# A block of three branches in emulated fp32: weights two chunks ahead, attention results summed where they arise, other load orders at four borders, last group in halves

## The chip, the cores and the metric

The kernel runs on one core of a Trainium2 chip. Times are device microseconds (us) of a whole execution. TensorE is called PE, VectorE DVE, ScalarE ACT, GpSimd POOL, and SyncE SP; SP here issues most loads, one queue in program order.

## The reference

One layer of a hybrid encoder, 512 positions by 2048 features, fp32:

```
h = rms_norm(x); proj = h @ w_in            # 2048 x 15424: all branch inputs and gates
conv_y = b * conv3(c * u);   o_conv = (conv_y * silu(conv_z)) @ w_conv_out
q = rms_norm(c_q) @ w_uq;  kv = rms_norm(c_kv) @ w_ukv   # 16 heads, chunk-causal attention
                             o_mla  = (mla_y * silu(mla_z)) @ w_mla_out
mem_y = cross-attention of 4 heads into 256 memory tokens
                             o_mem  = (mem_y * silu(mem_z)) @ w_mem_out
merged = sig(g_conv)*o_conv + sig(g_mla)*o_mla + sig(g_mem)*o_mem
out = x + merged @ w_o
```

## The kernel before

**Arithmetic.** A product in fp32 is made of three matmuls in fp32r (mm3, L158 to L163): high by high, low by high, high by low. So each operand is split into a high and a low part: ACT rounds the raw tile to the high part, DVE subtracts it for the low part. For activations the splits are made once; for weights they are made as they are streamed.

**Weights.** A weight chunk is loaded by SP into a raw tile (tag raw, 3 buffers of 8 KB a partition) and split into whi (ACT) and wlo (DVE), two buffers each. The wide matrices w_in, w_mla_out and w_o go through a fast scheme with 7 instead of 8 block products: pair_weights (L245 to L257) loads four blocks, makes three sums on DVE (L250 to L252), then whi (L254) and wlo (L255), each 128 x 1792. The activations need such sums too: pair_parts (L235 to L242), of a pair of feature blocks. One chunk is 42 matmuls of 256 columns (panel_steps); four chunks make a panel of 256 output features. The plain matrices (w_ukv, w_uq, w_conv_out, w_mem_out) go through plain_jobs and dense_units, at 384 or 512 columns, with splits at L154 and L155.

**Queue of jobs.** Every chunk is a job in one list. take (L172) runs the job of the chunk it returns and of the next: load, sums and splits of chunk n+1 are written into the program before the matmuls of chunk n.

**Order of the work.** The order of PE and SP is the order in which the program is written; for the other engines a scheduler picks among what is ready (in the first panels the order of DVE is written too). Streams of attention and projection are interleaved by strings such as ORDER_Q1 and ORDER_MEM, in which a letter or digit is a step of one stream and w a step of the projection.

**Stages**, by time in the profile:

- 0 to 115: keys and values of the memory tokens; norm of x and its pairs xp.
- 115 to 1355: 60 panels of w_in. A finished panel e is sent to DRAM (latdram, zdram, gdram and others) after its non-linearity; panel cq also gives the rotary keys.
- 1355 to 1650: the latent projections (w_ukv, w_uq) and attention of 16 heads, two heads a group. The latents come back from latdram as blk tiles; krh, krl, tabs, mask are small tables. attend multiplies a head's result by its gate z and stores it to aadram (L960, L961).
- 1600 to 1780: w_conv_out, with the attention into the memory tokens between its chunks.
- 1790 to 1955: panels of w_mla_out. Their activations xm are made by new_pairs (L1138): load from aadram into a raw tile, three sums, split.
- 1955 to 2044: w_mem_out in 4 groups of 512 features. mem_pair (L1190) merges two of its banks with the sum of the other branches and makes the pair xo: loads from gdram and mgdram into a raw tile, L1195 (product), L1196 (sum), three sums, split at L241 (ACT) and L242 (DVE).
- 2044 to the end: panels of w_o on the xo pairs.

Of the kernel before, what the change touches and what calls it, by code (L numbers as in the profile page):

```python
# [30 lines left out]
P = 128  # L31
S = 512
# [75 lines left out]
def body(ctx, tc, a, out):  # L108
# [63 lines left out]
    def take(ahead=1):  # L172
        for entry in queue[:1 + ahead]:
            if entry[1] is None:
                entry[1] = entry[0]()
        return queue.pop(0)[1]

    def plain_jobs(srcs, n, cut=False, parts=(), beside=None):
# [56 lines left out]
    def pair_parts(f, x):  # L235
# [3 lines left out]
        vec.tensor_tensor(out=f[:, 7], in0=f[:, 3], in1=f[:, 6], op=ALU.add)  # L239
        yield  # L240
        act.activation(x[:, 0], f[:, 1:8], AF.Copy)  # L241
        vec.tensor_tensor(out=x[:, 1], in0=f[:, 1:8], in1=r32(x[:, 0]), op=ALU.subtract)  # L242
        yield

    def pair_weights(src):  # L245
# [10 lines left out]
        return hi, lo  # L256

    later = []

    def panel_steps(xp, e, tag, middle=None):  # L260
# [5 lines left out]
        for c in range(nch):  # L266
# [6 lines left out]
            for kk in range(2):  # L273
# [81 lines left out]
    kr_ = const.tile([P, NTB], F32, name="kr_")  # L355
    pos_i = const.tile([P, NTB], I32, name="pos_i")
# [16 lines left out]
    aadram = dram.tile([NP, P, 2, S], F32, name="aadram")  # L373
# [238 lines left out]
    def rotary():  # L612
# [68 lines left out]
        krr = rstd_of(krss, NTB, 1.0 / 64, const)  # L681
# [19 lines left out]
        pool.tensor_tensor(out=kr_, in0=lmean[:, 0], in1=mhalf[:, :NTB], op=ALU.pow)  # L701
        yield
# [8 lines left out]
    def finish(n, e):  # L711
# [43 lines left out]
    queue.insert(next(at for at in range(len(queue)) if at == 12), [rotary_weights, None])  # L755
# [47 lines left out]
    tabs = pc.tile([P, 2, NTB, 64], F32, name="tabs")  # L803
# [89 lines left out]
    run("28w", w=first)  # L893

    def attend(head, h, qrb, kn, vs, qn, qd):
# [59 lines left out]
        z = pa.tile([P, S], F32, tag="z", name="z", bufs=2)  # L955
        nc.sync.dma_start(z, zdram[head // 2][:, head % 2])
# [3 lines left out]
        vec.tensor_tensor(out=z, in0=yb, in1=z, op=ALU.mult)  # L960
        nc.gpsimd.dma_start(aadram[head // 2][:, head % 2], z)  # L961
# [218 lines left out]
    for _ in work:  # L1180
        next(pairs, None)
# [139 lines left out]
```

## Time and profile before

| what | value |
|---|---|
| median of 3 runs | 2218.77 us (2218.43 to 2224.96) |
| profiled execution, own time | 2227.57 us |
| its span | 2225.8 us |
| mean granted clock of PE | 0.981 |
| PE / DVE / ACT / POOL busy | 2151.9 / 1746.5 / 1005.0 / 116.0 us |
| DMA | 328.02 MB, mean 147 GB/s |

The span is that of the profiled execution; the 1.8 us beside it lie around the first and last instruction. A row of a timeline is: start in us, duration in us, engine, line, operation, what it writes and reads, shape, count; in brackets the idle time of the engine before it and what ended that. A count over 1 merges neighbours, and the duration is then from the first start to the last end. SPq is SP's queue of DMA issues: the duration of an issue row is not that of the transfer.

### The profile page before, as it was taken

How to read it: one execution, taken by the hardware profiler on the slowest of the kernel's cores; microseconds unless marked ns; L12 is line 12 of the kernel's file. 1: busy time of each engine (PE TensorE's matmuls, PEld its weight loads, DVE VectorE, ACT ScalarE, POOL GpSimd, SP SyncE). 2: the span in 40 equal slices, each digit the busy share in tenths (PEclk: the TensorE clock that was granted, in tenths of full speed). 3: DMA queues.
4: the chain of work that ended last, by engine and by line, in shares of the span. 5: the costliest groups of instructions: out<-in, count | busy, mean ns of one | idle time of the engine just before them, and what ended most of it. 6: DMA issues, size and time to landing. Idle time of an engine off the chain costs nothing.

```text
span 2225.8 us, 38861 instructions
## 1 busy us (share of the span) xinstructions
PE 2151.9 (97%) x16040; PEld 2059.5 (93%) x16040; DVE 1746.5 (78%) x2759; ACT 1005.0 (45%) x1215; POOL 116.0 (5%) x157
## 2 busy tenths in 40 slices
PE   9989999999999999999999998999999879999998
PEld 8779999999999999999999997888888679987898
DVE  6866788888888888888888874788876778857886
ACT  6633344343344334444444444777765333323332
POOL 0000000000000000000000001222211100000000
PEclk9989999999999999999999999999999989999999
DMA  8533343343333334344444345222246746654443
GB/s 329 204 103 124 133 149 117 124 142 124 124 125 132 124 124 136 120 134 138 133 135 144 130 133 214 73 74 100 93 178 225 254 145 171 209 189 161 153 160 114
DMA packets 92993, 328.02 MB, mean 147 GB/s; under 512 B 10960, under 2 KB 11216, under 8 KB 90768
## 3 DMA queue, kind: packets, MB, share of 16 engines
q1 hardware_dynamic: 75600, 264.90, 35.5%
q0 software_dynamic: 8288, 35.39, 4.7%
q10 hardware_dynamic: 8928, 25.25, 3.2%
q8 instruction: 125, 2.05, 0.4%
q14 instruction: 52, 0.43, 0.1%
HBM read 270.19 MB, written 55.31 MB: 146 GB/s over the span
## 4 chain that ended last, share of the span: by engine, by line
PE 75%; DVE 8%; DMA 6%; issue 6%; ACT 3%; POOL 1%; SPq 0%; DVEq 0%; ACTq 0%; POOLq 0%
PE acc L162 13%; PE acc L161 13%; PE acc L163 13%; PE aux L162 10%; PE aux L163 10%; PE aux L161 10%; DVE wlo L255 3%; DMA raw<-in_w_o 1%; ACT whi L254 1%; DMA raw<-in_w_mla_out 1%; DMA raw<-in_w_h 1%; PE aux L943 1%; DVE wlo L155 1%; DVE raw L250 1%; DMA raw<-gdram 1%
## 5 line engine op out<-in xcount | busy, mean ns | idle before, releaser
L254 ACT ACTIVATE whi<-raw 128x1792 fp32r<-128x1792 f32 x304 | 517.5, 1703 | 792.9 <-PE acc L162 363.9
L255 DVE TENSOR_TENSOR wlo<-raw,whi 128x1792 fp32r<-128x1792 f32 x304 | 614.7, 2023 | 205.8 <-ACT whi L254 205.3
L161 PE MATMUL acc<-xp,whi 128*128 128x256 f32 (+1 forms) x1712 | 481.1, 281 | 5.5 <-ACT whi L254 3.2
L163 PE MATMUL acc<-xp,wlo 128*128 128x256 f32 (+1 forms) x1712 | 480.7, 281 | 3.1 <-DVE wlo L255 3.1
L162 PE MATMUL acc<-xp,whi 128*128 128x256 f32 (+1 forms) x1712 | 481.1, 281 | 0.0
L163 PE MATMUL aux<-xp,wlo 128*128 128x256 f32 x1680 | 471.3, 281 | 4.2 <-DVE wlo L255 3.8
L161 PE MATMUL aux<-xp,whi 128*128 128x256 f32 x1680 | 471.3, 281 | 1.2 <-ACT whi L254 1.2
L162 PE MATMUL aux<-xp,whi 128*128 128x256 f32 x1680 | 471.5, 281 | 0.0
L161 PEld LDWEIGHTS acc<-xp,whi 128*128 128x128 f32 (+1 forms) x1712 | 322.6, 188 | 6.2 <-ACT whi L254 3.6
L163 PEld LDWEIGHTS acc<-xp,wlo 128*128 128x128 f32 (+1 forms) x1712 | 321.5, 188 | 3.8 <-DVE wlo L255 3.7
L162 PEld LDWEIGHTS acc<-xp,whi 128*128 128x128 f32 (+1 forms) x1712 | 322.0, 188 | 0.0
L163 PEld LDWEIGHTS aux<-xp,wlo 128*128 128x128 f32 x1680 | 316.3, 188 | 5.6 <-DVE wlo L255 5.6
L161 PEld LDWEIGHTS aux<-xp,whi 128*128 128x128 f32 x1680 | 317.6, 189 | 1.5 <-ACT whi L254 1.4
L162 PEld LDWEIGHTS aux<-xp,whi 128*128 128x128 f32 x1680 | 317.1, 189 | 0.0
L250 DVE TENSOR_TENSOR raw<-raw 128x512 f32<-128x512 f32 x304 | 208.5, 686 | 58.3 <-DMA raw<-in_w_h 32.8
L155 DVE TENSOR_TENSOR wlo<-raw,whi 128x1024 fp32r<-128x1024 f32 (+2 forms) x87 | 101.3, 1165 | 53.0 <-ACT whi L154 53.0
L154 ACT ACTIVATE whi<-raw 128x1024 fp32r<-128x1024 f32 (+2 forms) x87 | 88.0, 1013 | 104.4 <-PE acc L162 43.9
L252 DVE TENSOR_TENSOR raw<-raw 128x256 f32<-128x256 f32 x304 | 128.1, 422 | 6.2
L251 DVE TENSOR_TENSOR raw<-raw 128x256 f32<-128x256 f32 x304 | 128.0, 421 | 5.7
L161 PE MATMUL acc<-whi,blk 128*128 128x384 f32 (+1 forms) x224 | 86.3, 385 | 7.6 <-ACT whi L154 7.6
L319 POOL TENSOR_TENSOR rs_r<-rs_t,mhalf 128x2 f32<-128x2 f32 (+2 forms) x71 | 70.0, 997 | 313.6 <-DVE rs_t L318 199.4
L162 PE MATMUL acc<-wlo,blk 128*128 128x384 f32 (+1 forms) x224 | 82.0, 366 | 0.3 <-DVE wlo L155 0.3
(345 smaller groups left out, 3922.8 us busy)
## 6 DMA issues: line engine op xcount, KB each, us to landing
raw<-in_w_h SPq DMA_DIRECT2D x240, 512.0 KB, 3.5
raw<-in_w_mla_out SPq DMA_DIRECT2D x32, 512.0 KB, 3.6
raw<-in_w_o SPq DMA_DIRECT2D x32, 512.0 KB, 3.8
raw<-in_w_mem_kv SPq DMA_DIRECT2D x31, 512.0 KB, 7.5
gdram<-e ACTq DMA_DIRECT2D x24, 512.0 KB, 2.9
raw<-in_w_ukv SPq DMA_DIRECT2D x16, 512.0 KB, 4.9
raw<-in_w_conv_out SPq DMA_DIRECT2D x16, 512.0 KB, 6.1
raw<-in_w_mem_out SPq DMA_DIRECT2D x16, 512.0 KB, 4.5
```

The costliest lines, as they stand in the source:

```text
L154: act.activation(hi[:, cols], raw[:, cols], AF.Copy)
L155: vec.tensor_tensor(out=lo[:, cols], in0=raw[:, cols], in1=r32(hi[:, cols]), op=ALU.subtract)
L161: nc.tensor.matmul(o, lhsT=s[0], rhs=m[0], start=start, stop=False, skip_group_check=shared)
L162: nc.tensor.matmul(o, lhsT=s[0], rhs=m[1], start=False, stop=False, skip_group_check=shared)
L163: nc.tensor.matmul(o, lhsT=s[1], rhs=m[0], start=False, stop=stop, skip_group_check=shared)
L250: vec.tensor_tensor(out=f[:, 4:6], in0=f[:, 1:3], in1=f[:, 0:1].to_broadcast([P, 2, 256]), op=ALU.add)
L251: vec.tensor_tensor(out=f[:, 6], in0=f[:, 5], in1=f[:, 1], op=ALU.add)
L252: vec.tensor_tensor(out=f[:, 7], in0=f[:, 6], in1=f[:, 3], op=ALU.add)
L254: act.activation(hi, f[:, 1:8], AF.Copy)
L255: vec.tensor_tensor(out=lo, in0=f[:, 1:8], in1=r32(hi), op=ALU.subtract)
L319: pool.tensor_tensor(out=r, in0=t, in1=mhalf[:, :n], op=ALU.pow)
L943: nc.tensor.transpose(out=b[:, i * P:(i + 1) * P], in_=ps[i][:, j * P:(j + 1) * P], identity=ident)
```

## The change

- **take** keeps two steps per job: load and sums of chunk n+2 are written ahead of the splits of chunk n+1 (jobs are generators with two yields).
- **Rotary keys** (rotary_keys_raw) move from the end of panel cq to the middle of the next panel, on the other bank tag; the weights w_kr go from place 12 to 15 of the list. mqs and mqn, constants for the memory queries, are made in that stage and no more in the memory attention.
- **Border to the latents:** krh, krl, tabs, mask and w_uq are loaded ahead of the last two latent blocks; ORDER_Q1 and ORDER_MEM are rewritten.
- **Latent results:** z is one tile for two heads (one buffer), the three sums of a pair are made there, and the 7 blocks (128 x 1792) are stored to aadram. new_pairs loads them into the xm tile and splits in place: no raw tile, no sums.
- **w_mem_out** runs in groups of 512, 512, 512, 256 and 256; mem_pair has a tile mg of its own (one buffer) in place of a raw tile.

The core of the diff:

```diff
     def take(ahead=1):
-        for entry in queue[:1 + ahead]:
+        for at, entry in enumerate(queue[:2 + ahead]):
             if entry[1] is None:
                 entry[1] = entry[0]()
-        return queue.pop(0)[1]
+                entry.append(next(entry[1]))
+            if at <= ahead and entry[2] is None:
+                entry[2] = next(entry[1])
+        return queue.pop(0)[2]
...
+            if c == 2:
+                while between:
+                    between.pop(0)("aux" if tag == "acc" else "acc")
...
             if i == 0:
-                rotary_keys_raw("acc")
+                between.append(rotary_keys_raw)
...
-    run("4w", w=first)
-    for n in (6, 7):
-        latent(n)
     nc.sync.dma_start(r32(krh), krdram[:, 0])
...
-    run("28w", w=first)
+    run("9w", w=first)
+    for n in (6, 7):
+        latent(n)
+    run("23w", w=first)
...
-        z = pa.tile([P, S], F32, tag="z", name="z", bufs=2)
-        nc.sync.dma_start(z, zdram[head // 2][:, head % 2])
+        if h == 0:
+            z = pa.tile([P, 8, H], F32, tag="z", name="z", bufs=1)
+            nc.sync.dma_start(two(z), zdram[head // 2])
...
-        nc.gpsimd.dma_start(aadram[head // 2][:, head % 2], z)
+        if h == 1:
+            pair_sums(z)
+            nc.gpsimd.dma_start(aadram[head // 2], z[:, 1:8])
...
-            x, t = pair_tile(px, f"xm{n}"), raw_tile()
-            nc.sync.dma_start(flat(t[:, 0:4]), aadram[n].rearrange("p f n -> p (f n)"))
+            x = pair_tile(px, f"xm{n}")
+            nc.sync.dma_start(r32(x[:, 1]), aadram[n])
             xp.append(x)
-            yield from pair_parts(t, x)
+            yield
+            pair_split(r32(x[:, 1]), x)
+            yield
...
-    for grp in range(4):
+    for grp in range(3):
         upcoming(*plain_jobs([a["w_mem_out"][grp][c] for c in range(4)], 512))
+    for grp in range(2):
+        upcoming(*plain_jobs([a["w_mem_out2"][grp][c] for c in range(4)], 256))
...
     def mem_pair(n, banks):
-        t = raw_tile()
+        t = pm.tile([P, 8, H], F32, tag="mg", name="mg", bufs=1)
...
-    for grp in range(4):
-        if grp == 3:
+    for tag, width in (("acc", 512), ("aux", 512), ("acc", 512), ("aux", 256), ("aux", 256)):
+        if done == 7:
             work = panels(xp, a["w_o"], 8, lambda n: make_o(n), lambda n, e: finish_o(n, e))
```

How the order moves at three places. Lines shift by a few: L249, L250 to L252, L255 and L242 of before are L262, L263 to L265, L269 and L250 of the change.

DVE in the first panels of w_in, before. e is a pair of x being scaled (L458) and summed (L236 to L239), raw the weights:

```order
L255 TENSOR_TENSOR wlo<-raw,whi 128x1792
L458 TENSOR_TENSOR e<-e,xscale 128x1024
L236 TENSOR_TENSOR e<-e 128x512
L237 SCALAR_TENSOR_TENSOR e<-e 128x256
L239 TENSOR_TENSOR e<-e 128x256
L250 TENSOR_TENSOR raw<-raw 128x512
```

And the change:

```order
L269 TENSOR_TENSOR wlo<-raw,whi 128x1792
L263 TENSOR_TENSOR raw<-raw 128x512
L264 TENSOR_TENSOR raw<-raw 128x256
L265 TENSOR_TENSOR raw<-raw 128x256
L477 TENSOR_TENSOR e<-e,xscale 128x1024
L243 TENSOR_TENSOR e<-e 128x512
L244 SCALAR_TENSOR_TENSOR e<-e 128x256
```

The sums of the next weights stand right behind the split, and the four operations on x behind them.

SP at the border from the panels to the latents, before:

```order
L795 DMA blk<-latdram 128x1024 x8
L889 DMA krh<-krdram 128x512
L890 DMA krl<-krdram 128x512
L891 DMA tabs<-csdram 128x512
L892 DMA mask<-in_mask 128x512
L191 DMA raw<-in_w_uq 128x768 x2
```

And the change:

```order
L822 DMA blk<-latdram 128x1024 x6
L913 DMA krh<-krdram 128x512
L914 DMA krl<-krdram 128x512
L915 DMA tabs<-csdram 128x512
L916 DMA mask<-in_mask 128x512
L196 DMA raw<-in_w_uq 128x768 x2
L822 DMA blk<-latdram 128x1024 x2
```

Two blocks go behind w_uq. The semaphore of the last gate panel's write (DMAHW0), on which the seventh block waited, is waited for by krl in the change.

SP from the memory output to w_o, before (gdram and mgdram are the loads of a merge pair; the rows start with the last w_mem_out load):

```order
L191 DMA raw<-in_w_mem_out 128x1024 x2
L1192 DMA raw<-gdram 128x1024
L1193 DMA raw<-mgdram 128x1024
L249 DMA raw<-in_w_o 128x1024 x2
L1192 DMA raw<-gdram 128x1024
L1193 DMA raw<-mgdram 128x1024
```

And the change:

```order
L196 DMA raw<-in_w_mem_out 128x512 x4
L1225 DMA mg<-gdram 128x1024
L1226 DMA mg<-mgdram 128x1024
L1225 DMA mg<-gdram 128x1024
L1226 DMA mg<-mgdram 128x1024
L262 DMA raw<-in_w_o 128x1024 x3
```

The first three loads of w_o follow the loads of the sixth and seventh merge pair, where before the first two followed those of the sixth alone.

## Rows read from the trace of the kernel before

**Rows 1.** The page: busy time of PE, and the groups of weight splits and weight sums of the panels (busy us in all, mean ns of one, idle time before them).
```profile
PE 2151.9 (97%) x16040; PEld 2059.5 (93%) x16040; DVE 1746.5 (78%) x2759; ACT 1005.0 (45%) x1215; POOL 116.0 (5%) x157
...
L254 ACT ACTIVATE whi<-raw 128x1792 fp32r<-128x1792 f32 x304 | 517.5, 1703 | 792.9 <-PE acc L162 363.9
L255 DVE TENSOR_TENSOR wlo<-raw,whi 128x1792 fp32r<-128x1792 f32 x304 | 614.7, 2023 | 205.8 <-ACT whi L254 205.3
...
L250 DVE TENSOR_TENSOR raw<-raw 128x512 f32<-128x512 f32 x304 | 208.5, 686 | 58.3 <-DMA raw<-in_w_h 32.8
...
L252 DVE TENSOR_TENSOR raw<-raw 128x256 f32<-128x256 f32 x304 | 128.1, 422 | 6.2
```

**Rows 2.** Busy time by stage: stretch, its length, busy us (and instructions) of PE, PEld, DVE, ACT, POOL, the granted clock of PE, DMA share, GB/s.
```profile
115.00:225.00 110.00, 97.28 (x719) 94.95 (x719) 75.53 (x99) 40.42 (x37) 1.94 (x4) 0.89 0.32 106
225.00:1355.00 1130.00, 1128.72 (x9588) 1127.99 (x9587) 935.05 (x1293) 474.80 (x360) 11.86 (x20) 1.00 0.41 134
...
1430.00:1650.00 220.00, 217.71 (x1257) 194.17 (x1256) 179.10 (x515) 166.57 (x405) 51.67 (x60) 1.00 0.30 102
1750.00:1800.00 50.00, 34.05 (x154) 27.96 (x153) 40.61 (x49) 17.11 (x13) 4.35 (x8) 0.83 0.68 242
1960.00:2040.00 80.00, 80.00 (x355) 66.26 (x354) 51.92 (x59) 24.65 (x20) 0.85 (x1) 1.00 0.56 190
2040.00:2140.00 100.00, 89.25 (x688) 86.67 (x687) 81.16 (x106) 34.03 (x24) 0.00 (x0) 0.95 0.45 148
```

**Rows 3.** The same table for short stretches at the borders.
```profile
125.00:175.00 50.00, 40.62 (x284) 38.99 (x283) 38.30 (x49) 17.79 (x15) 0.00 (x0) 0.86 0.21 66
215.00:220.00 5.00, 4.77 (x27) 4.77 (x28) 1.72 (x4) 0.00 (x0) 0.00 (x0) 0.66 0.35 105
1370.00:1380.00 10.00, 4.84 (x14) 4.44 (x15) 1.92 (x2) 3.12 (x8) 0.00 (x0) 0.50 0.92 349
...
1690.00:1700.00 10.00, 7.99 (x36) 6.33 (x35) 8.97 (x27) 8.34 (x24) 1.56 (x2) 0.83 0.74 286
...
1930.00:1940.00 10.00, 8.22 (x55) 7.81 (x54) 7.91 (x15) 3.67 (x3) 0.00 (x0) 0.83 0.42 152
2060.00:2070.00 10.00, 9.19 (x56) 9.19 (x57) 7.46 (x10) 1.71 (x1) 0.00 (x0) 0.68 0.62 205
```

**Rows 4.** Waits of PE between 205 and 225 (who waited for whom: us in total, times, longest). L570 is a sum of the rotary keys.
```profile
PE acc L161 <- DVE e L570: 2.3, 1, 2.3
```

**Rows 5.** Timeline of SP's queue at the border to the latents: the eight block loads, and w_uq.
```profile
1341.90 22.65 SPq L795 DMA_DIRECT2D blk<-latdram  x8
...
1367.09 0.92 SPq L191 DMA_DIRECT2D raw<-in_w_uq  x2
```

**Rows 6.** Timeline of PE there: the first matmul that reads w_uq.
```profile
1374.85 0.69 PE L161 MATMUL acc<-whi,blk 128*128 128x384 f32 x1 [7.58 <-ACT whi L154]
```

**Rows 7.** Timeline of SP's queue in the attention: three loads of z.
```profile
1466.35 0.33 SPq L956 DMA_DIRECT2D z<-zdram  x1
...
1479.17 0.33 SPq L956 DMA_DIRECT2D z<-zdram  x1
...
1501.45 0.33 SPq L956 DMA_DIRECT2D z<-zdram  x1
```

**Rows 8.** DMA issues by tile: count, KB each, median us from issue to landing.
```profile
latdram<-e POOLq DMA_DIRECT2D x4, 1024.0 KB, 5.2
...
am<-amdram SPq DMA_DIRECT2D x8, 512.0 KB, 8.0
```

**Rows 9.** Waits of PE between 1680 and 1800. p L1102 is the memory queries' scaling, whi L154 here w_conv_out, whi L254 and wlo L255 w_mla_out.
```profile
PE acc L161 <- ACT whi L254: 9.9, 1, 9.9
PE aux L161 <- ACT whi L154: 3.2, 1, 3.2
PE acc L163 <- DVE wlo L255: 2.6, 1, 2.6
PE aux L326 <- DVE p L1102: 2.0, 2, 1.5
```

**Rows 10.** Timeline of SP's queue between 1720 and 1800.
```profile
1728.62 15.33 SPq L1141 DMA_DIRECT2D raw<-aadram  x2
1750.91 0.81 SPq L191 DMA_DIRECT2D raw<-in_w_conv_out  x2
...
1758.06 0.81 SPq L191 DMA_DIRECT2D raw<-in_w_conv_out  x2
...
1778.41 14.76 SPq L249 DMA_DIRECT2D raw<-in_w_mla_out  x4
```

**Rows 11.** Timeline of SP's queue between 2018 and 2066: the first w_o loads, and the load of the seventh merge pair.
```profile
2031.49 6.27 SPq L249 DMA_DIRECT2D raw<-in_w_o  x2
2043.53 0.33 SPq L1192 DMA_DIRECT2D raw<-gdram  x1
```

**Rows 12.** Timeline of DVE between 1980 and 2060: the split of the first merge pair, and product and sum of the seventh.
```profile
1985.58 2.02 DVE L242 TENSOR_TENSOR xo<-raw,xo 128x1792 fp32r<-128x1792 f32 x1
...
2046.99 1.29 DVE L1195 TENSOR_TENSOR raw<-aux,raw 128x512 f32<-128x512 f32 x2 [0.88 <-DMA raw<-gdram]
2048.32 1.23 DVE L1196 TENSOR_TENSOR raw<-raw 128x1024 f32<-128x1024 f32 x1
```

**Rows 13.** Timeline of PE there: the first matmul of the w_o panels.
```profile
2044.21 0.28 PE L161 MATMUL acc<-xo,whi 128*128 128x256 f32 x1
```

More of the change, by code (lines that the diff above doesn't have):

```diff
@@ L255, in pair_weights @@
         vec.tensor_tensor(out=lo, in0=f[:, 1:8], in1=r32(hi), op=ALU.subtract)
-        return hi, lo
-    later = []
+        yield hi, lo
+    later, between = [], []
     def panel_steps(xp, e, tag, middle=None):
@@ L355, in body @@
     kr_ = const.tile([P, NTB], F32, name="kr_")
+    mqs = const.tile([P, 16], F32, name="mqs")
+    mqn = const.tile([P, 16], F32, name="mqn")
     pos_i = const.tile([P, NTB], I32, name="pos_i")
@@ L701, in rotary @@
         pool.tensor_tensor(out=kr_, in0=lmean[:, 0], in1=mhalf[:, :NTB], op=ALU.pow)
+        mqr = rstd_of(sums[:, 4:8].rearrange("p a b -> p (a b)"), 16, 1.0 / M, pe)
+        vec.tensor_scalar(out=mqs, in0=mqr, scalar1=MEM_SCALE, scalar2=None, op0=ALU.mult)
+        vec.tensor_scalar(out=mqn, in0=mqr, scalar1=-MEM_SCALE, scalar2=None, op0=ALU.mult)
         yield
@@ L754, in body @@
     work = panels(xp, a["w_h"], len(SEQUENCE), make, finish, "aux")
-    queue.insert(next(at for at in range(len(queue)) if at == 12), [rotary_weights, None])
+    queue.insert(next(at for at in range(len(queue)) if at == 15), [rotary_weights, None])
     for grp in range(NG):
@@ L783, in body @@
     pc, close_c = open_pool("lat", "right")
+    PLACES = ((2, 3), (6, 7), (4, 5), (0, 1))
     def block(n):
-        t = ph.tile([P, 2, S], F32R, tag="blk" if n < 6 else "bll", name="blk", bufs=6 if n < 6 else 2)
+        t = ph.tile([P, 2, S], F32R, tag=f"blk{n // 2}", name="blk", bufs=2)
         return t, (t[:, 0], t[:, 1])
-    blocks = {n: block(n) for n in (6, 7, 0, 1, 2, 3, 4, 5)}
+    blocks = {n: block(n) for two_ in PLACES for n in two_}
     ckT = [blocks[n][1] for n in range(4)]
@@ L1059, in body @@
     pg, close_g = open_pool("gate", "right")
-    mqr = rstd_of(sums[:, 4:8].rearrange("p a b -> p (a b)"), 16, 1.0 / M, pq)
-    mqs = pq.tile([P, 16], F32, name="mqs")
-    mqn = pq.tile([P, 16], F32, name="mqn")
-    vec.tensor_scalar(out=mqs, in0=mqr, scalar1=MEM_SCALE, scalar2=None, op0=ALU.mult)
-    vec.tensor_scalar(out=mqn, in0=mqr, scalar1=-MEM_SCALE, scalar2=None, op0=ALU.mult)
     mv = [None] * 4
@@ L1187, in body @@
     xp = [pair_tile(px, f"xo{i}") for i in range(NP)]
+    pm, close_m = open_pool("merge", "right")
     pam2, close_am2 = open_pool("actm2", "left")
     def mem_pair(n, banks):
-        t = raw_tile()
+        t = pm.tile([P, 8, H], F32, tag="mg", name="mg", bufs=1)
         nc.sync.dma_start(two(t, 4), gdram[16 + n])
@@ L1194, in mem_pair @@
         for i in range(2):
-            vec.tensor_tensor(out=two(t, 4)[:, i], in0=banks[2 * (n % 2) + i], in1=two(t, 4)[:, i], op=ALU.mult)
+            vec.tensor_tensor(out=two(t, 4)[:, i], in0=banks[i], in1=two(t, 4)[:, i], op=ALU.mult)
         vec.tensor_tensor(out=two(t), in0=two(t), in1=two(t, 4), op=ALU.add)
@@ L1198, in mem_pair, with mem_pairs @@
         yield from pair_parts(t, xp[n])
-    def mem_pairs(grp, banks):
-        for n in (2 * grp, 2 * grp + 1):
-            yield from mem_pair(n, banks)
+    def mem_pairs(n, banks):
+        for i in range(len(banks) // 2):
+            yield from mem_pair(n + i, banks[2 * i:2 * i + 2])
     late_blocks = []
@@ L1221, in body @@
             pass
-        pairs = mem_pairs(grp, banks)
+        pairs = mem_pairs(done, banks)
+        done += width // 256
     close_am2()
```

57 lines of the change are left out of this document (36 added, 21 removed).

## The prediction

> **What bounds the kernel now.** I read the page first, then the table by stage, then short stretches, then waits and queues. The page says that TensorE (PE) is the limit: busy 97% of the span [rows 1]. The table shows where it is not [rows 2]. In the panels, 225 to 1355, PE is busy 1128.72 of 1130 us at full clock, and no edit there can pay. The pace is 9588 matmuls in 1130 us, 8.49 per us, so a chunk of 42 takes 4.95 us. What is lost lies at the borders: 12.7 us idle in the first panels, 16 us idle around 1775, 10.8 us idle at the start of the last panels, and a lower granted clock after each. At clock 0.50 one microsecond of PE does half a microsecond of work, so a stretch is judged by idle time and clock together [rows 3].
>
> **The profiled execution** took 2227.57 us, 0.4% above the 2218.77 us of the median. I take the sum from the former and carry it over by the ratio 0.996. About 0.3% (6.7 us) is what a measurement of this kernel tells from no change.
>
> **First panels, sums two chunks ahead.** Between 125 and 175, 284 matmuls ran; at 8.49 per us that is 33.5 us of work, so 16.5 us are lost, in idle time and at a clock of 0.86 [rows 3]. In the order before, VectorE (DVE) does four operations on x between one weight split and the next chunk's sums; in the new order the sums follow the split. The operations stay the same, DVE is busy 38.3 of these 50 us [rows 3], so the gain cannot exceed 11.7 us. I take half, **6**, as the x operations still stand before some splits; ends 3 and 11.7.
>
> **Rotary keys inside the next panel.** In 215 to 220 the clock is 0.66 after a wait for the rotary sums [rows 3]: 1.7 us of clock; the wait before it is 2.3 us [rows 4]. Set between matmuls of a running panel, on the other banks, the wait has cover of its own chunk (4.95 us). **+4**; ends 0 (it waits there too) and 4. The constants for memory queries, moved into the same stage, cost a few small operations under PE-bound panels: nothing. Without that cover they would cost under a microsecond.
>
> **Panels to latents.** SP's row of eight block loads lasts from 1341.90 to 1364.55, as the seventh waits for the last gate panel's write; w_uq is issued at 1367.09 [rows 5], and PE stands 7.58 us until 1374.85 [rows 6]. In the new order two block loads go behind w_uq, but krl now carries the wait on that DMA semaphore, so w_uq still stands behind the write. It gains the issue time (krl at about 1363.7 and three issues: 1364.9, so 2.2 us) and 1.3 MB of transfers that went ahead of it or with it (two blocks and krh), at 349 GB/s [rows 3] 3.7 us more. The ends are 2.2 and 5.9. I take **4.5**, between them, since w_uq has its own landing time to serve. The new mix of projection and attention steps behind it: no row prices it, ends -1 and +3, taken as nothing.
>
> **Attention.** The three sums of a pair (0.69 + 0.42 + 0.42 = 1.53 us by the same shapes in rows 1) come in here, 8 times, 12 us of DVE; DVE is busy 179 of 220 us and PE 217.7 [rows 2], so cover is there. It would cost up to 12 us if none of it were hidden. More doubtful is z: one buffer for a pair where each head had one of two. Its reload must wait for the store. In the trace the queue's z issues are 1466.35, 1479.17 and 1501.45 [rows 7]: each follows the store of an earlier head, and a pair's second product lies 22.3 us before the next pair's first. The new chain is 1.53 of sums, a store of 0.9 MB (5.2 us for 1 MB on the same queue) and a load of 1 MB (8.0 us where six of 0.5 MB queue) [rows 8]: 14.7 us, below 22.3. So the row says no wait. The Trainium skill, "Trainium Kernel Development and Optimization", Best Practices, asks for two buffers to overlap DMA with compute, which speaks against this step; by it each pair would stand for its reload, and the sum would turn to a loss (the size is in rival 4). No wait of this kind can show in a trace that has two buffers; the gap of 22.3 us speaks for the row. I take **-1** for crowding; ends -6 and +1.
>
> **Conv and memory attention.** In 1690 to 1700 PE is busy 7.99 us at clock 0.83 [rows 3]; the p operations it waits for [rows 9] need mqs or mqn, which now exist long before. 2.0 idle (10 - 7.99) and 1.4 of clock: **+3**; ends 1 and 3.7.
>
> **Latent results: sums gone, no raw tile.** Before, the loads of the attention results take raw tiles, and SP is stuck behind them: issues from 1728.62 last 15.33 us, w_conv_out follows at 1750.91, w_mla_out at 1778.41 [rows 10]. PE pays 3.2 us for w_conv_out, then 9.9 and 2.6 for w_mla_out [rows 9]. In the change the pairs load straight into place, so those loads wait for no weight buffer, and DVE loses 8 x 1.53 = 12.2 us of work where it is busy 40.6 of 50 us [rows 2]. But the loads grow from 4.2 to 7.3 MB. Ahead of the first w_mla_out chunk now stand four loads of 0.92 MB and two of 0.52, with it 5.2 MB: at the 349 GB/s of rows 3 15 us, at the 242 GB/s of rows 2 21.7. They stand behind the last w_conv_out load, which before was issued at 1758.06 [rows 10]; from about 1760 on it lands between 1775 and 1782; with 1.53 of sums, 1.70 of whi and 2.02 of wlo [rows 1] PE runs on at 1780 to 1787 instead of 1792.9. Gain 6 to 13; **+10**, ends 3 and 16 (with all three waits gone).
>
> **Latents' output to memory output.** 1930 to 1940: 1.8 idle and 1.7 of clock [rows 3], where the block loads for the next stage go ahead of w_mla_out. With weights one chunk further ahead this has 4.95 us more cover: **+3**; ends 0 and 3.5.
>
> **Merge and w_o: the part that goes the other way.** Before, the merge pairs share the three raw tiles. Now they have one tile of their own, so pair n+1 is loaded when pair n is split. One round is the load (issued 2043.53 [rows 11], its product on DVE at 2046.99 [rows 12]: 3.46), 1.29 + 1.23 for product and sum [rows 12], 1.53 for the three sums, 1.70 for the high part, 2.02 for the split [rows 1]: 11.2 us. PE gives a pair every 10.8 us (48 matmuls of 80 us / 355 [rows 2]). So the merges run at the chain's pace, not PE's. The first split before starts at 1985.58 [rows 12] and ends 2.0 later; with five rounds of 11.2 to 12.5, as weight splits stand between, the sixth ends at 2043 to 2050, 2047 taken. The new order has the load of the seventh pair ahead of the first three w_o loads. So w_o is issued after 2047 where it was 2031.49 [rows 11]. PE finishes the memory output at 2044.21, as before [rows 13]. Behind the issue come, on DVE and ACT in that order, the seventh pair's operations (3.46 + 2.52 + 1.53, some 2 of w_o's sums between them, 1.70 for its high part), then whi 1.70: PE restarts near 2060; wlo stands behind that pair's 2.02 split, near 2063. Idle 16 + 3, half clock after it (2060 to 2070 had 0.68 after a shorter stop [rows 3]) 2.5, and 2.5 for small waits: 24. Before, the stretch lost 10.75 idle and 0.05 x 100 = 5 of clock [rows 2], some 15.5. **-8.5**; ends -15 (13.5 us a round) and +2 (chain hidden). Halving the last group frees the seventh pair 11 us sooner; the chain uses none of it.
>
> **Sum.** 6 + 4 + 4.5 - 1 + 3 + 10 + 3 - 8.5 = 21. 2227.6 - 21 = 2206.6, times 0.996: **2198**.
>
> **Rivals.**
> 1. *The last stage does not stall* (0.17). The order puts w_o behind the merge, but if rounds take 10 us the sixth split ends at 2038 and w_o comes in time. Against it: five durations of rows 12 and 1 add to 11.2. The loss of 15.5 then shrinks too: gain 28 to 38, 2181 to 2191.
> 2. *The border at 1775 is a transfer bound* (0.13). 3.1 MB more in a stretch that already moved 242 GB/s; w_mla_out comes when it came. Gain 8 to 13: 2206 to 2211.
> 3. *The change does little of what it says* (0.12): w_uq still behind the gate write, DVE in the first panels full anyway, the rotary wait only moved; with the loss at w_o these leave -6 to 8: 2211 to 2225.
> 4. *Slower by the z tile* (0.08): the second buffer is gone, so a pair waits by what its chain exceeds 22.3 us, and w_ukv and w_uq queue behind the load. It decides from there: at 26.5 us (store and load 1.9 times the 13.2 of rows 8) seven pairs lose 29 and the sum is -8: 2227. The rule on two buffers in the Trainium skill's "Trainium Kernel Development and Optimization", Best Practices, has it so.
> My forecast has 0.50: gain 14 to 28, 2191 to 2205.
>
> **How the numbers follow.** Faster: the forecast, rivals 1 and 2, and a quarter of 3: 0.83. Same: the rest of 3 and an eighth of 4: 0.10. Slower: the rest of 4, 0.07. The range leaves out the far end of rival 1 and what is slower: 2178 to 2219. Even if all lower ends came together, 3 + 0 + 2.2 - 6 + 1 + 3 + 0 - 15 = -12, it would be slower; all upper ends, 49 gained; neither is likely.
>
> **What would show it.** First panels: 125 to 165 with clock near 1 and short waits on wlo. No wait on the rotary sums. w_uq landing near 1370 (less what came before). PE's restart on xm some 10 us sooner than the earlier gains explain. At the last border, the load of the seventh merge pair issued when the sixth split ends, w_o right behind it, and PE idle 15 to 20 us: without that stop the largest negative term is wrong. z's load waiting on its store with PE standing on the product would show rival 4; a full DMA share up to PE's restart on xm, rival 2.

## The result, and the profile after

The changed kernel takes 2199.05 us (median of 6 runs, 2195.98 to 2209.17); the kernel before, in 6 runs, 2223.24. The ratio is 0.9898, 95% interval 0.9872 to 0.9925: faster by 1.0%. The forecast was 2198, a ratio of 0.9906. The profiled execution took 2199.24 us with a span of 2197.4, 28.4 less than that of before, whose profiled execution took 4 us more than the median of its kernel.

PE's busy time fell by 20 us to 2132.2 with the same matmuls: of the 28.4 us, 19.7 are matmuls that ran at a higher clock and 8.7 are idle time (page of the changed kernel, section 1):

```profile
PE 2132.2 (97%) x16040; PEld 2043.9 (93%) x16040; DVE 1744.8 (79%) x2763; ACT 1004.2 (46%) x1219; POOL 110.8 (5%) x149
```

To see where, I take the same matmul as a milestone in both timelines of PE and compare the time between milestones. Those of after that closed a wait (start, duration, and in brackets the idle time and its releaser), which answer to [rows 6, 13] and the waits of [rows 9]:

```profile
1350.92 0.69 PE L161 MATMUL acc<-whi,blk 128*128 128x384 f32 x1 [3.60 <-ACT whi L154]
...
1753.55 0.58 PE L161 MATMUL acc<-xm,whi 128*128 128x256 f32 x1 [7.45 <-ACT whi L268]
1755.75 0.58 PE L163 MATMUL acc<-xm,wlo 128*128 128x256 f32 x1 [1.40 <-DVE wlo L269]
...
2026.65 0.58 PE L161 MATMUL acc<-xo,whi 128*128 128x256 f32 x1 [16.02 <-ACT whi L268]
2029.49 0.58 PE L163 MATMUL acc<-xo,wlo 128*128 128x256 f32 x1 [2.04 <-DVE wlo L269]
```

| from, to (us between the matmuls) | before | after | gain | forecast |
|---|---|---|---|---|
| span's start, first panel matmul | 115.28 | 107.59 | +7.7 | not priced |
| that, first latent matmul | 1240.91 | 1228.66 | +12.2 | +10 (6 + 4) |
| that, first w_uq matmul | 18.66 | 14.67 | +4.0 | +4.5 |
| that, first L163 of w_mla_out | 418.02 | 404.83 | +13.2 | +12 (-1 + 3 + 10) |
| that, first w_mem_out matmul | 164.27 | 166.37 | -2.1 | +3 |
| that, last w_o matmul | 262.41 | 269.42 | -7.0 | -8.5 |
| all | 2219.55 | 2191.54 | +28.0 | +21 |

Four of the five forecasts stand within 2.2 us. One row was left out of the forecast, and one has the wrong sign. Two rows share a gain, though. At the first w_uq matmul PE has just stood still and runs at a low clock (0.50 in [rows 3]), so the cost of that stop goes on into the next row. From the last panel matmul to the first attention product, with the same matmuls in all kernels, the stretch shows the whole border, before and after (columns as in [rows 2]):

```profile
1356.07:1425.04 68.97, 58.03 (x277) 51.01 (x276) 39.20 (x113) 38.77 (x90) 13.62 (x14) 0.88 0.35 127
...
1336.13:1397.59 61.46, 55.27 (x278) 48.58 (x276) 37.72 (x106) 38.20 (x89) 13.93 (x14) 0.94 0.40 144
```

Cut there, the border gains 7.5 us, and the stretch from the first attention product to the first L163 of w_mla_out 9.7 (367.8 to 358.2).

The last row is the stop that the prediction put at w_o. SP's queue after shows the order that made it: the seventh pair's load is issued when the sixth split (2012.24 + 2.02) is done, and w_o right behind it, at 2015.13 (start, duration of the issue, line, tile, count; answers to [rows 11]):

```profile
2014.29 0.32 SPq L1225 DMA_DIRECT2D mg<-gdram  x1
2014.65 0.43 SPq L1226 DMA_DIRECT2D mg<-mgdram  x1
2015.13 1.40 SPq L262 DMA_DIRECT2D raw<-in_w_o  x3
```

DVE's splits of the merge pairs show the chain in front of it: 13.8, 13.1, 12.0, 12.0, 12.3 and 12.9 us from one to the next (DVE's timeline after, answers to the first of [rows 12]; the forecast was 11.2 to 12.5):

```profile
1949.12 2.03 DVE L250 TENSOR_TENSOR xo<-mg,xo 128x1792 fp32r<-128x1792 f32 x1 [1.77 <-ACT xo L249]
1962.88 2.03 DVE L250 TENSOR_TENSOR xo<-mg,xo 128x1792 fp32r<-128x1792 f32 x1 [0.37 <-ACT xo L249]
1975.95 2.03 DVE L250 TENSOR_TENSOR xo<-mg,xo 128x1792 fp32r<-128x1792 f32 x1 [0.64 <-ACT xo L249]
1987.93 2.02 DVE L250 TENSOR_TENSOR xo<-mg,xo 128x1792 fp32r<-128x1792 f32 x1 [1.77 <-ACT xo L249]
1999.94 2.03 DVE L250 TENSOR_TENSOR xo<-mg,xo 128x1792 fp32r<-128x1792 f32 x1 [1.17 <-ACT xo L249]
2012.24 2.02 DVE L250 TENSOR_TENSOR xo<-mg,xo 128x1792 fp32r<-128x1792 f32 x1 [1.76 <-ACT xo L249]
2025.15 2.02 DVE L250 TENSOR_TENSOR xo<-mg,xo 128x1792 fp32r<-128x1792 f32 x1
```

The short stretches after (length, busy us and instructions of PE, PEld, DVE, ACT, POOL, PE clock, DMA share, GB/s): 125 to 175 answers to the first of [rows 3], with clock 0.98 for 0.86 and DVE busy 45 of 50; the last is the stop at w_o, 16.6 us idle, with a mean granted clock of 0.69 over the stretch.

```profile
125.00:175.00 50.00, 44.06 (x356) 42.95 (x356) 45.07 (x61) 21.92 (x18) 1.31 (x2) 0.98 0.36 119
...
70.00:90.00 20.00, 20.00 (x92) 16.26 (x91) 18.57 (x20) 16.79 (x22) 0.00 (x0) 1.00 0.77 282
2008.00:2028.00 20.00, 3.43 (x14) 2.36 (x12) 14.55 (x22) 6.38 (x4) 0.00 (x0) 0.69 0.36 131
```

And 70 to 90 is the row that the forecast left out, in the keys and values of the memory. Before, the same stretch had 55 matmuls at clock 0.83 for 92 now (and 92 in e1 below):

```profile
70.00:90.00 20.00, 15.76 (x55) 11.80 (x54) 14.57 (x16) 12.78 (x17) 0.00 (x0) 0.83 0.81 305
```

### The profile page after: what moved, and what is told of

It is laid out like the page before. It is cut to its first block, busy times and chain, and to the rows that moved or that the text cites. A ratio compares the mean times of both kernels' runs of the same rounds, so it can differ in the third digit from the quotient of the medians.

```text
span 2197.4 us, 38848 instructions
## 1 busy us (share of the span) xinstructions
PE 2132.2 (97%) x16040; PEld 2043.9 (93%) x16040; DVE 1744.8 (79%) x2763; ACT 1004.2 (46%) x1219; POOL 110.8 (5%) x149
## 4 chain that ended last, share of the span: by engine, by line
PE 84%; DVE 7%; DMA 5%; ACT 3%; issue 1%; POOL 0%; SPq 0%; DVEq 0%; POOLq 0%; ACTq 0%
PE acc L161 15%; PE acc L163 15%; PE acc L162 15%; PE aux L161 12%; PE aux L163 12%; PE aux L162 12%; DVE wlo L269 2%; DMA sb<-gdram 1%; DMA raw<-in_w_h 1%; PE aux L970 1%; DMA amdram<-my 1%; DVE raw L263 1%; PE aux L953 1%; DMA raw<-in_w_mla_out 0%; PE aux L954 0%
## 5 line engine op out<-in xcount | busy, mean ns | idle before, releaser
L268 ACT ACTIVATE whi<-raw 128x1792 fp32r<-128x1792 f32 x304 | 517.4, 1703 | 796.3 <-PE acc L162 363.1
L269 DVE TENSOR_TENSOR wlo<-raw,whi 128x1792 fp32r<-128x1792 f32 x304 | 614.6, 2022 | 205.4 <-ACT whi L268 205.0
L163 PE MATMUL aux<-xp,wlo 128*128 128x256 f32 (+1 forms) x1712 | 479.8, 280 | 4.8 <-DVE wlo L269 4.7
L161 PE MATMUL aux<-xp,whi 128*128 128x256 f32 (+1 forms) x1712 | 480.7, 281 | 0.1
L162 PE MATMUL aux<-xp,whi 128*128 128x256 f32 (+1 forms) x1712 | 479.4, 280 | 0.0
L163 PE MATMUL acc<-xp,wlo 128*128 128x256 f32 x1680 | 469.5, 279 | 3.4 <-DVE wlo L269 3.4
L161 PE MATMUL acc<-xp,whi 128*128 128x256 f32 x1680 | 470.1, 280 | 0.0
L162 PE MATMUL acc<-xp,whi 128*128 128x256 f32 x1680 | 469.1, 279 | 0.0
L163 PEld LDWEIGHTS aux<-xp,wlo 128*128 128x128 f32 (+1 forms) x1712 | 321.3, 188 | 5.7 <-DVE wlo L269 5.7
L161 PEld LDWEIGHTS aux<-xp,whi 128*128 128x128 f32 (+1 forms) x1712 | 321.1, 188 | 0.5 <-ACT whi L268 0.5
L162 PEld LDWEIGHTS aux<-xp,whi 128*128 128x128 f32 (+1 forms) x1712 | 320.4, 187 | 0.0
L163 PEld LDWEIGHTS acc<-xp,wlo 128*128 128x128 f32 x1680 | 315.4, 188 | 4.4 <-DVE wlo L269 4.4
L161 PEld LDWEIGHTS acc<-xp,whi 128*128 128x128 f32 x1680 | 315.3, 188 | 0.0
L162 PEld LDWEIGHTS acc<-xp,whi 128*128 128x128 f32 x1680 | 314.7, 187 | 0.0
L263 DVE TENSOR_TENSOR raw<-raw 128x512 f32<-128x512 f32 x304 | 208.4, 686 | 46.9 <-DMA raw<-in_w_h 32.4
L154 ACT ACTIVATE whi<-raw 128x1024 fp32r<-128x1024 f32 (+2 forms) x91 | 89.0, 978 | 105.5 <-PE acc L162 37.2
L265 DVE TENSOR_TENSOR raw<-raw 128x256 f32<-128x256 f32 x304 | 128.3, 422 | 6.3
```

The source lines that it names most:

```text
L154: act.activation(hi[:, cols], raw[:, cols], AF.Copy)
L161: nc.tensor.matmul(o, lhsT=s[0], rhs=m[0], start=start, stop=False, skip_group_check=shared)
L162: nc.tensor.matmul(o, lhsT=s[0], rhs=m[1], start=False, stop=False, skip_group_check=shared)
L163: nc.tensor.matmul(o, lhsT=s[1], rhs=m[0], start=False, stop=stop, skip_group_check=shared)
L263: vec.tensor_tensor(out=f[:, 4:6], in0=f[:, 1:3], in1=f[:, 0:1].to_broadcast([P, 2, 256]), op=ALU.add)
```

## The experiments

Theory: the gain is a sum of local waits, each removed or made by its own edit. Rivals stand with each run. Each has 4 to 6 executions, and its ratio is to the kernel before. The times between the milestones of the table, from each run's profile; a column is the time from the milestone before it:

| kernel | panel | latent | w_uq | w_mla_out | w_mem_out | end | ratio (95%) |
|---|---|---|---|---|---|---|---|
| before | 115.3 | 1240.9 | 18.7 | 418.0 | 164.3 | 262.4 | 1 |
| the change | 107.6 | 1228.7 | 14.7 | 404.8 | 166.4 | 269.4 | 0.9898 (0.9872, 0.9925) |
| e1 two ahead only | 107.1 | 1242.0 | 12.9 | 412.4 | 167.5 | 260.0 | 0.9942 (0.9927, 0.9956) |
| e2 groups undone | 108.5 | 1229.2 | 15.5 | 407.2 | 167.8 | 260.7 | 0.9873 (0.9855, 0.9891) |
| e3 w_o first | 107.7 | 1229.9 | 14.2 | 407.4 | 168.3 | 270.5 | 0.9918 (0.9902, 0.9934) |
| e4 second merge tile | 109.7 | 1230.5 | 15.3 | 404.5 | 166.8 | 256.4 | 0.9856 (0.9837, 0.9874) |
| e5 blocks spread | 107.3 | 1226.9 | 14.3 | 405.7 | 162.6 | 268.4 | 0.9895 (0.9877, 0.9913) |
| e6 w_uq first | 108.4 | 1229.2 | 10.9 | 405.8 | 167.4 | 271.2 | 0.9889 (0.9873, 0.9905) |
| e7 results undone | 107.7 | 1227.5 | 15.8 | 409.5 | 167.7 | 269.6 | 0.9931 (0.9917, 0.9946) |
| e8 together | 109.0 | 1227.5 | 10.9 | 405.8 | 163.0 | 256.2 | 0.9817 (0.9789, 0.9846) |

Stages that an edit does not touch repeat within 2 to 4 us, which is how far a difference in this table can be trusted. What e5, e6 and e7 do to their stages (3.8, 3.8 and 4.6 us) is close to that, so it rests on the waits shown with them as well.

**e1, weights two chunks ahead, by itself** (on the kernel before; jobs made generators as in the change):

```diff
-        for entry in queue[:1 + ahead]:
+        for at, entry in enumerate(queue[:2 + ahead]):
             if entry[1] is None:
                 entry[1] = entry[0]()
+                entry.append(next(entry[1]))
+            if at <= ahead and entry[2] is None:
+                entry[2] = next(entry[1])
...
```

> The kernel before with one edit: load and sums of the weights two chunks ahead (take and the jobs as generators). Theory (the gain is a sum of local waits, each removed by its own edit): the first panel matmul comes at 107 to 109 instead of 115.28, the first latent matmul 12 to 18 us earlier than before's 1356.19 (7.7 ahead of the panels, 4 to 10 in the first panels; the rotary wait of 2.3 us stays), then nothing: PE still waits 9.9 + 2.6 us for w_mla_out. In all 0.992 to 0.995 of before. Rival (prefetch two chunks ahead is the whole change, the rest is neutral): 0.988 to 0.990, and the waits for w_uq and w_mla_out shrink too.

Measured: 0.9942, inside what the theory expected and off the rival's. The first panel matmul comes at 107.06, so the 7.7 us ahead of the panels are this edit's. The first latent matmul comes at 1349.04, 7 us earlier than before, where 12 to 18 were expected. The panels and the next column must be read together: e1's waits of PE around the border (who for whom, total, times, longest; two answers, 107 to 225 and 1320 to 1365) have

```profile
PE acc L161 <- DVE e L576: 2.3, 1, 2.3
...
PE aux L161 <- DMA blk<-latdram: 9.3, 1, 9.3
```

The first is the rotary wait of [rows 4], still there. The second was not expected: two ahead puts the w_ukv loads earlier in SP's queue, but the first of the block loads behind them is now the one held by the gate panel's write, to 1344.86, and PE waits 9.3 us at the first latent matmul instead of 7.6 at w_uq. Without it the panels take 1232.7 us, 8.2 less than before. From the last panel matmul to the first attention product e1 takes 66.4 us, with the wait for the block in it, for 69.0 before:

```profile
1339.48:1405.92 66.44, 54.68 (x278) 47.74 (x276) 38.23 (x109) 38.16 (x90) 13.83 (x14) 0.92 0.50 182
```

So the wait is moved rather than removed, and the border is no worse for it. At w_mla_out PE waits 14.3 + 3.0 us, for 9.9 + 2.6 before, and restarts 364.7 us after the first attention product, for 364.4 before: the edit does nothing there but bring PE sooner.

**e2, the last stage undone** (four groups of 512, merge pairs in raw tiles):

```diff
-        t = pm.tile([P, 8, H], F32, tag="mg", name="mg", bufs=1)
+        t = raw_tile()
...
-    for tag, width in (("acc", 512), ("aux", 512), ("acc", 512), ("aux", 256), ("aux", 256)):
-        if done == 7:
+    for tag, width in (("acc", 512), ("aux", 512), ("acc", 512), ("aux", 512)):
+        if done == 6:
```

> The changed kernel with its last edit undone: w_mem_out in four groups of 512, and the merge pairs in raw tiles again. Theory (the one merge tile makes a chain in front of the w_o loads): the stop of 16.0 + 2.0 us at the first w_o matmuls goes, w_o is loaded before the sixth split ends; small waits of some 10 us in the first w_o panels as before; 3 to 8 us faster than the changed kernel, ratio to before 0.986 to 0.989. Rival (the halves and the own tile pay, the stop is paid back by what is then free of waits): the same or slower than the changed kernel, 0.990 to 0.993.

Measured: 0.9873; the last stage falls by 8.8 us to 260.7, and w_o is issued at 2004.36, 13 us ahead of PE's need. So by the stage this part of the change costs what the prediction said, 7 to 9 us; the medians of the whole differ by 5.1.

**e3, w_o ahead of the seventh merge load:**

```diff
-            if n % 4 == 3:
+            if n % 4 == 3 and (done < 7 or n == 15):
                 next(pairs, None)
```

> The changed kernel with the load of the seventh merge pair written behind the first two w_o loads instead of ahead of the first three; merge tile and halves stay. Theory (w_o is late only because its loads queue behind a load that waits for the sixth split): w_o is issued some 10 to 13 us earlier, right behind the sixth pair's load, PE's stop of 18 us falls below 4, and the whole is 12 to 18 us faster than the changed kernel: ratio 0.981 to 0.985. Rival (ACT and DVE are behind with the merges, so whi and wlo come late whatever is loaded): the stop stays above 10 us or comes back as waits at the fourth chunk of the first panels; ratio 0.987 to 0.990.

Measured: 0.9918, no gain; the last stage takes 270.5. Here the theory fell and the rival's mechanism held, though the time came out above the 0.987 to 0.990 that it named. w_o is issued at 2008.11 and the one stop is gone, but it is cut in three, 14.3 us in all for 18 (PE's timeline of e3):

```profile
2018.64 0.39 PE L161 MATMUL acc<-xo,whi 128*128 128x256 f32 x1 [2.74 <-ACT whi L268]
2020.70 0.38 PE L163 MATMUL acc<-xo,wlo 128*128 128x256 f32 x1 [1.55 <-DVE wlo L269]
...
2034.83 0.58 PE L161 MATMUL acc<-xo,whi 128*128 128x256 f32 x1 [2.68 <-ACT whi L268]
2037.24 0.58 PE L163 MATMUL acc<-xo,wlo 128*128 128x256 f32 x1 [1.62 <-DVE wlo L269]
...
2047.56 0.39 PE L161 MATMUL aux<-xo,whi 128*128 128x256 f32 x1 [3.43 <-ACT whi L268]
2050.36 0.58 PE L163 MATMUL aux<-xo,wlo 128*128 128x256 f32 x1 [2.31 <-DVE wlo L269]
```

ACT's timeline of e3 says why for the second: ACT sits idle 9.72 us for the seventh pair's sums, since its high part (L249) stands ahead of the third whi in the order of ACT's program. At the third stop it is the same with the eighth pair, 9.45 us.

```profile
2031.49 1.70 ACT L249 ACTIVATE xo<-mg 128x1792 fp32r<-128x1792 f32 x1 [9.72 <-DVE mg L246]
2033.10 1.68 ACT L268 ACTIVATE whi<-raw 128x1792 fp32r<-128x1792 f32 x1
```

So the load order was one of two places where w_o stands behind the merges; ACT's and DVE's order is the other. The prediction had named both; the expectation of e3 forgot the second.

**e4, a second merge tile** (the second, fourth and sixth pair in a raw tile):

```diff
-        t = pm.tile([P, 8, H], F32, tag="mg", name="mg", bufs=1)
+        t = raw_tile() if n in (1, 3, 5) else pm.tile([P, 8, H], F32, tag="mg", name="mg", bufs=1)
```

> The changed kernel with the second, fourth and sixth merge pair in a raw tile, so that a pair's load need not wait for the split of the pair just before it; the order of loads stays. Theory (one tile makes the rounds 12 us long): splits follow PE's pace, the sixth ends some 5 to 10 us sooner after the first, w_o is issued with the seventh pair's load one round earlier, the stop of 18 us falls to 0 to 8: ratio 0.982 to 0.987. Rival (rounds are set by DVE, ACT and weight splits, or by raw tiles that the merges now take from w_mem_out): ratio 0.989 to 0.993 with new waits on w_mem_out.

Measured: 0.9856; the last stage takes 256.4, 13.1 us less than the change and 6 less than before. The splits come in twos at PE's pace (DVE's timeline of e4; the fifth and sixth). The sixth comes 45.3 us after the first, for 63.1 in the change, 18 sooner where 5 to 10 were expected:

```profile
2000.04 2.02 DVE L250 TENSOR_TENSOR xo<-mg,xo 128x1792 fp32r<-128x1792 f32 x1 [0.36 <-ACT xo L249]
2001.98 2.02 DVE L250 TENSOR_TENSOR xo<-raw,xo 128x1792 fp32r<-128x1792 f32 x1
```

With e2 and e3 this settles it: the chain through the one tile made the loss, not the halves and not the load order alone. With the chain cut, halves and an own tile beat the stage as it was before (262.4) and e2, which has neither but loads two ahead (260.7).

**e5, the blocks of w_mem_out spread** over three panels:

```diff
-            if n == 6:
-                for k in range(6):
+            if 2 <= n < 5:
+                for k in (2 * n - 4, 2 * n - 3):
```

> The changed kernel with the six block loads (3 MB, for w_mem_out) given out two at a time in the third to fifth panel of w_mla_out instead of all in the seventh. Theory (the stop of 3.2 + 1.3 us at 1904 is w_mla_out landing 14 us after its issue behind that burst): first w_mla_out matmul to first w_mem_out matmul falls from 166.4 to 159 to 162 us, ratio to before 0.987 to 0.989. Rival (the sums of a later chunk now stand before the split on DVE, and that makes the stop, burst or not): 164 to 167 us, ratio 0.989 to 0.991.

Measured: the stage falls from 166.4 to 162.6, just above the theory's 159 to 162, and the wait of 3.2 us is gone: the burst delays w_mla_out. The waits of the stage add up to 1.5 us less (5.9 to 4.4); the rest comes with the clock, 0.98 for 0.97 over the stage. The ratio, 0.9895, cannot tell 4 us from the change's own interval. PE's waits in this stage, after:

```profile
PE aux L161 <- ACT whi L268: 3.2, 1, 3.2
PE acc L163 <- DVE wlo L269: 1.4, 1, 1.4
PE aux L163 <- DVE wlo L269: 1.3, 1, 1.3
```

and in e5 (in both, 1.4 us are the first L163 of the stage):

```profile
PE aux L163 <- DVE wlo L269: 2.4, 3, 1.9
PE acc L163 <- DVE wlo L269: 2.0, 2, 1.4
```

**e6, w_uq ahead of the tables:**

```diff
     first = project(0, res, "aux", "acc")
+    run("1w", w=first)
...
-    run("9w", w=first)
+    run("8w", w=first)
```

> The changed kernel with the first w_uq loads ahead of krh, krl, tabs and mask, so that only the second half of w_uq stands at the semaphore of the last gate panel's write. Theory (w_uq is late because krl holds the queue until that write has landed): w_uq issued near 1331 instead of 1344.74, PE's wait of 3.6 us goes, and the low clock after it; latents to first w_uq matmul from 14.7 to 10.9 to 11.5 us, 4 to 6 us in all, ratio 0.987 to 0.989. Rival (the raw tile or the bandwidth sets when w_uq lands): stage within 1 us of 14.7, ratio 0.989 to 0.991.

Measured: 10.9 us to w_uq, PE's wait gone, as the theory said; 0.9889 in all, so again within the interval of the change. From the last panel matmul to the first attention product it takes 56.0 us, for 61.5 in the change, at full clock. SP's queue shows the first half issued at once and the second held until the gate panel's write has landed:

```profile
1327.70 17.48 SPq L196 DMA_DIRECT2D raw<-in_w_uq  x2
```

```profile
1337.50:1393.52 56.02, 52.76 (x278) 46.15 (x277) 37.62 (x106) 38.02 (x90) 13.40 (x14) 1.00 0.44 155
```

**e7, the latent results undone** (z per head, four blocks stored, raw tiles and sums ahead of w_mla_out):

```diff
...
-            x = pair_tile(px, f"xm{n}")
-            nc.sync.dma_start(r32(x[:, 1]), aadram[n])
+            x, t = pair_tile(px, f"xm{n}"), raw_tile()
+            nc.sync.dma_start(flat(t[:, 0:4]), aadram[n].rearrange("p f n -> p (f n)"))
...
```

> The changed kernel with the latent results as before: one z per head, 4 blocks stored, and loads through a raw tile with sums and splits ahead of w_mla_out. Theory (raw tiles and the sums hold up w_conv_out and w_mla_out): first w_uq matmul to first w_mla_out L163 matmul rises from 404.8 to 412 to 416 us, PE waits again over 10 us for w_mla_out; ratio to before 0.993 to 0.996. Rival (the gain there is from weights two chunks ahead and the moved constants): 404 to 408 us, ratio 0.989 to 0.991.

Measured: 0.9931; the stage rises by 4.6 us to 409.5, between the two expectations. The waits show that two things happen. PE's waits from w_uq to w_mla_out, after:

```profile
PE acc L161 <- ACT whi L268: 7.5, 1, 7.5
...
PE aux L343 <- DVE p L1130: 3.0, 1, 3.0
...
PE acc L163 <- DVE wlo L269: 1.4, 1, 1.4
```

and in e7:

```profile
PE acc L161 <- ACT whi L268: 14.8, 1, 14.8
...
PE acc L163 <- DVE wlo L269: 3.1, 1, 3.1
```

Undone, w_mla_out is waited for 9.0 us longer, but much of that is PE arriving sooner: the wait on p, 3.0 us, is not there. In the change DVE does the second memory head's mk splits (1662.51) ahead of the first head's maxima (1663.21), and a wlo of w_conv_out (1666.04) ahead of the first p (1668.36); in e7 the maxima are at 1660.97, the first p at 1663.86, and both other works come after. That wait answers to the 2.0 us of [rows 9], which the prediction took as gone. It stands at 3.0 us in all seven other traces that have the latent results edit.

What the edit is worth is how much sooner PE restarts: the 4.6 us. And it is not the queue that gives it. w_mla_out is issued at 1743.03 in the change and at 1743.04 in e7, both 392.1 us after the first w_uq matmul. In e7 the pair loads hold the queue; in the change a load of the gate does, which waits for the write of sb to mgdram. SP's queue, its wait, and two stretches of the change (columns as in [rows 2]):

```profile
1738.86 4.06 SPq L1018 DMA_DIRECT2D sb<-gdram  x2
1743.03 15.29 SPq L262 DMA_DIRECT2D raw<-in_w_mla_out  x5
...
SPq L1018 <- DMA mgdram<-sb: 14.2, 2, 10.9
...
1725.00:1735.00 10.00, 10.00 (x45) 8.26 (x45) 8.06 (x8) 4.47 (x3) 2.17 (x4) 1.00 1.01 403
1735.00:1743.00 8.00, 8.00 (x37) 6.60 (x37) 5.28 (x3) 5.46 (x4) 0.00 (x0) 1.00 1.02 416
```

and in e7:

```profile
1726.54 14.54 SPq L1164 DMA_DIRECT2D raw<-aadram  x4
...
1743.04 19.64 SPq L262 DMA_DIRECT2D raw<-in_w_mla_out  x5
...
1735.00:1743.00 8.00, 6.75 (x30) 5.26 (x28) 6.43 (x8) 2.83 (x2) 0.00 (x0) 1.00 0.32 94
```

In the change the DMA engines are full there (a share of 1.01 and 1.02), and at 0.88 from there to PE's restart, which is nearly the sign that the prediction named for its rival 2. After the issue DVE begins the sums of w_mla_out at 1750.03 in the change and at 1752.25 in e7, where the pairs' own sums and splits go first.

**e8, three edits together** (e4, e5 and e6 on the change):

> The changed kernel with three edits: second merge tile from the raw tiles (ratio 0.9856 by itself), block loads spread, w_uq first. Theory (the waits lie in different stages and add): 0.9856 less 5 us and 5 us: 0.980 to 0.983. Rival (what is won at one border is given back at the next): 0.984 to 0.986.

Measured: 0.9817 (0.9789 to 0.9846), 2181.42 us, in the range of the theory, with an interval that just reaches the rival's. The stages settle it: w_uq falls by 3.8 us, w_mem_out by 3.4 and the last by 13.2, as in e6, e5 and e4 (3.8, 3.8 and 13.0). The waits lie in different stages and add. It is 0.8% below the changed kernel and 1.8% below the kernel before.

## Why the prediction was right, and where not

- **First panels and rotary (10; 12.2 measured).** e1 gives 8.2 to two chunks ahead, where 6 was taken, under the bound of 11.7 that DVE's load set; the other 4.0 come with the remaining edits, and the 2.3 us wait that e1 keeps is gone in the change. The step held; the move of the rotary keys has no run of its own.
- **Not priced (0; 7.7).** The prediction went through the borders that the diff names and passed over the keys and values of the memory, though take serves them as well. The windows at 70 to 90 would have shown 4.2 us idle at clock 0.83. e1 has the gain, so it is the weights two ahead. It is the largest term missing from the sum, and it is a part left out, not a mechanism.
- **Border to the latents (4.5; 4.0, and 7.5 with the low clock behind it).** w_uq was issued 8.5 us after the first latent matmul for 10.9 before, 2.4 sooner (2.2 forecast), and e6 shows that krl held it. The forecast priced PE's stop and not the clock behind it, though [rows 3] show 0.50 there. Of the 7.5 us, 2.5 come with two ahead alone (e1: 66.4 for 69.0, no more than stages repeat by), the other 5.0 with the rest of the border's edits, the order of loads and the blocks' places among them; e6 shows 5.5 more to be had from that order.
- **Attention (-1; none seen).** In the 215 us from 1425 before and 1401 after, PE did 1224 matmuls in both, busy 212.71 and 212.67. The z tile costs nothing. Its chain was oversized: the load is 0.5 MB (the prediction has 1 MB) and lands in 3.9 us, the store in 4.0; with the sums 9.4 us, where 14.7 was taken, against a gap of 22.3. The rule that rival 4 took from the Trainium skill ("Trainium Kernel Development and Optimization", Best Practices: two buffers) did not bind here; e4 shows it binding at the merge tile, where a round (12 to 13.8) is longer than PE's pace (10.8).
- **Memory queries (+3; 4.8 from before to e7).** From the first attention product to the first L163 of w_mla_out before takes 367.8 us, e1 368.5, e7 363.1 and the change 358.2. So what e7 has and e1 lacks (the moved constants, the new order strings) is worth some 5 us; no run tells the constants from the order. The step "need mqs or mqn, which now exist long before" holds in e7, where no wait on p is left. In the change the next in line on DVE was other work, and PE waited 3.0 us for p.
- **Latent results (+10; 4.9 by the same figures of e7 and the change).** The failing step: "from about 1760 on it lands between 1775 and 1782", that is 17 to 24 us behind the last w_conv_out load. In the change it was 26.8 us from that load (1723.25) to the first sums (1750.03). The pairs wait for no raw tile, but w_mla_out is issued no sooner for it, since the queue stands behind the gate's load while the larger pair loads fill the DMA engines, much as rival 2 had it. PE waits 7.5 + 1.4 us there, for 9.9 + 2.6 before. The gain that is left follows DVE's lighter work by the traces; no run has the sums moved with the loads left alone. That this row came to 13.2 for 12 is luck: 3.5 us of clock from the border before it stand in it.
- **To w_mem_out (+3; -2.1).** The failing step is "With weights one chunk further ahead this has 4.95 us more cover". A load is issued when one of three raw tiles falls free, and that is no sooner for being written sooner: after the burst the first load was issued at 1884.98, 16.0 us before PE stood still for it, for 15.6 before (1918.44). It was summed at 1899.07, 14.1 us after the issue, for 12.3 before (1930.72), and its whi began 3.4 us later, for 1.8, as DVE took the next chunk's sums in between. The latter is what e5's rival said, though only behind the burst: e1 has the loss too (167.5), e5 removes it.
- **Merge and w_o (-8.5; -7.0).** Right in place, cause and size: rounds of 12 to 13.8 for the 11.2 to 12.5 taken, w_o behind the seventh load, 16.0 + 2.0 us idle for 16 + 3.

The sum fell 7 us short in the profiles (28.0 for 21): 7.7 left out, 5.1 too much at w_mem_out, the rest within 2.2 each way. So part of the agreement is luck: terms missed on either side cancel. By the ratio, 0.9898 for 0.9906, it looks closer than it was, since the profiled execution of before lay above its median; and carried over from the median of 6 runs of before (2223.24) in place of 3 (2218.77) the forecast would have been 2202, not 2198. Two slips in the sums change nothing: the upper ends add up to 47.8, not 49, and what the stretch at w_o lost before is 15.75, not 15.5.

## What to carry to other kernels

Go through every stage that a shared helper serves, not only those the diff names. A prefetch written earlier gains nothing where the buffer it fills is the last thing to fall free. A load that is freed of one wait gains nothing where the next one in its queue ends as late. Set milestones where the clock is full again, or one border's cost is booked to the next row. And where a chain through one tile takes as long as a stage's work or longer, look on every engine's order, not only the load queue's, for what stands behind the chain; moving one of them (e3) gains nothing.

## What the runs showed that was not expected

In the change and in e6 a DMA on SP's queue waits for a write on ACT's whose data it does not touch, because the program gives the DMAs of both queues completion semaphores in rotation, and the two have the same one. The write is that of the last gate panel (gdram). SP's own waits show which load is caught, in the changed kernel krl:

```profile
SPq L914 <- DMA gdram<-e: 11.5, 1, 11.5
```

in e6 the second half of w_uq:

```profile
SPq L196 <- DMA gdram<-e: 16.8, 1, 16.8
```

and in e1 the first of six latent blocks, with the other five behind it:

```profile
SPq L801 <- DMA gdram<-e: 19.6, 1, 19.6
```

In e1 the reason is not shown: by its records the block waits on that write's semaphore but completes on another. The memory that it takes over is a candidate; the changed kernel also gives the blocks other places (PLACES in its code), and no run has that alone. Either way a load added or moved well ahead changes which one waits, and what that costs depends on what stands behind it: 9.3 us of PE in e1, 3.6 in the change, none in e6.
